# Matmul minus matrix on one core: the last store in three transfers, and the order of SyncE's closing waits

## The chip, the cores and the metric

The kernel runs on one core of one Trainium2 chip. The metric is the device time of one execution in microseconds (us): 209.77 us for the kernel before, as the median of three runs (209.74 to 209.87). The profile is that of one execution; its span, from the first to the last instruction, is 208.0 us, and the run that it was taken of is given with 209.83 us.

## What is computed

```python
x         = (16, 512, 1024) float32
weight    = (1024, 768) float32
sub_value = (16, 512, 768) float32
out = (np.matmul(x, weight) - sub_value).astype(np.float32)
```

So 8192 rows of 1024 are multiplied by one weight, and a matrix of the result's size is subtracted. About 87 MB pass through the DMA engines: x and sub_value in, the result out.

## The kernel before

**Tiles.** The 8192 rows are cut in 64 m tiles of 128 rows. They lie in segments of eight m tiles: within a segment, partition p holds the eight neighbouring rows 8p to 8p+7, and tile j takes row 8p+j of each partition. A transfer of n m tiles therefore moves n x 4,096 bytes of x, or n x 3,072 bytes of sub_value or result, for each of the 128 partitions, as one contiguous piece each.

**Stages.** For each m tile ScalarE casts x to float16 (`cast`, L328), TensorE or VectorE transposes it (L346 and L359, or L379), TensorE multiplies it with the weight in 16 matmuls of 384 columns (`matmuls`, recorded at L199), and VectorE subtracts in place (`finish`, L428): the ring `so_ring` holds sub_value before, and the result after.

**Transfers.** The list `TRANSFERS` orders all loads and stores by hand: `('o', 56, 5), ('o', 61, 2), ('o', 63, 1)` are its last three, the stores of m tiles 56 to 60, of 61 and 62, and of 63. `issue` (L244) works it off whenever a cast or a subtraction is done in program order, and puts every transfer on SyncE's queue, with one exception: the last store is not issued there, but is kept in `outside` (L300).

**Completion.** Every transfer on SyncE takes a semaphore from `lane` (L232), called lane0, lane1 and so on. A lane is used again when it is `known` that all its earlier transfers have landed, because something that was waited for implies it.

**The end.** The instructions are given out engine by engine (L523 to L529) inside a first section that ends with a barrier of the engines. A second section (L532) belongs to SyncE: it waits for every lane whose transfers aren't known to have landed. There are seven of them, of which lane6, the last made, is that of the store of 61 and 62. The build puts them on wait instructions that carry two semaphores each, with the engines' own closing semaphores as partners; the first one is recorded at L535, the others at L567. Behind the section stands the last store, of m tile 63: 128 partitions of 3,072 bytes, issued by ScalarE (L537). `add_manual_dep` puts it behind the section in the order of the program without a semaphore (`NoSync`): as built, its issue waits for the end of the first section, and not for the lanes. SyncE then waits for the last store's own semaphore in a drain, and a closing barrier of all engines ends the program.

Of the kernel before, what the change touches and what calls it, by code (L numbers as in the profile page):

```python
# [8 lines left out]
P = 128  # L9
# [95 lines left out]
def kernel(  # L105
# [7 lines left out]
    nc = tc.nc  # L113
# [7 lines left out]
    n_mt = M_TOT // P  # L121
# [47 lines left out]
    def count(name):  # L169
# [13 lines left out]
        out=along, data0=ones, data1=ones, initial=0.0, op0=mybir.AluOpType.mult, op1=mybir.AluOpType.add,  # L183
    ), waits=[(counter["ident"], 1)], then=count("ident"))
    dve.add(lambda: nc.vector.transpose(across, along), waits=[(counter["ident"], 3)], then=count("ident"))  # L185
    for a in range(P // Q):
        here = slice(a * Q, (a + 1) * Q)
        dve.add(lambda here=here: nc.vector.tensor_tensor(  # L188
            out=ident[here, here], in0=along[here], in1=across[here], op=mybir.AluOpType.is_equal,
# [37 lines left out]
    lanes = []  # L227
    of_x, of_s, of_o = {}, {}, {}
    known = set()
# [300 lines left out]

    section.close()
    with tc.tile_critical(sync_engine=mybir.EngineType.SP, no_gpsimd_drain=True) as waited:  # L532
        for one in lanes:
            if not one["tags"] <= known:
                nc.sync.wait_ge(one["sem"], one["value"])  # L535
    here, there = outside
    stored = nc.scalar.dma_start(out=here, in_=there)  # L537
    tc.add_manual_dep(
        stored.ins, waited.name, mybir.DependencyInfo(mybir.DependencyClass.NoSync, mybir.DependencyReason.DATA),
        reason="behind the waits",  # L540
    )


# [28 lines left out]
```

## Time and profile before

| What | Value |
|---|---|
| time, median of 3 | 209.77 us |
| span of the profiled execution | 208.0 us |
| last subtraction (L428) | 201.44 to 202.40 us |
| last store, issue on ScalarE (L537) | 202.65 us, 0.36 us |
| last store, issue to landing | 4.5 us |
| store of m tiles 61 and 62, issue (L308) | 199.83 us |
| the same, issue to landing | 6.4 us |
| mean DMA rate over the span | 419 GB/s |

The page gives each engine's busy time and share, then the span in 40 slices with the busy share in tenths, where the DMA row is the mean over the core's 16 DMA engines. The chain that ended last is followed back from the last instruction. For an end of a few microseconds these are too coarse: there the timeline, the busy time by stretches that one sets oneself, and the view of what SyncE waited for are to be read. Register, branch, semaphore and DMA-issuing instructions are not counted as busy; a name such as SPq or ACTq is the queue of SyncE or ScalarE.

### The profile page before, as it was taken

The page shows a single profiled execution, that of the slowest core. Times are in us where ns is not written, and L with a number is a line of the kernel's source. Part 1 is how long each engine was busy: PE and PEld are TensorE (multiplying, and loading weights), DVE is VectorE, ACT ScalarE, POOL GpSimd, SP SyncE. Part 2 cuts the span into 40 slices and gives each one's busy share as a digit, 9 for nine tenths or more (in the row PEclk, how much of TensorE's full clock was granted, in tenths as well). Part 3 has the DMA queues.
Part 4 walks back from the last instruction along what each step waited for, and adds up shares of the span by engine and source line. Part 5 has one row for each costly group of instructions (what it writes and reads, how often), then busy time and mean ns, then how long its engine had stood idle before and what let it go on. Part 6 is the DMA issues. An engine that isn't in the chain of part 4 may idle for free.

```text
span 208.0 us, 2608 instructions
## 1 busy us (share of the span) xinstructions
PE 196.5 (94%) x1233; PEld 75.4 (36%) x701; DVE 127.8 (61%) x224; ACT 113.5 (55%) x113; POOL 1.0 (0%) x7
## 2 busy tenths in 40 slices
PE   6989699999999999999999999999999999999970
PEld 0133334333434433443443443344344344334410
DVE  2321516946894795598399379469839937943330
ACT  3274688616673861945745586293664738607300
POOL 1000000000000000000000000000000000000000
PEclk9999999999999999999999999999999999999997
DMA  6999999999999999999999999999999999999993
GB/s 224 405 430 428 429 428 432 443 427 433 449 411 473 376 454 435 463 410 408 474 422 416 421 435 449 405 471 395 444 441 433 428 411 449 444 416 425 423 420 164
DMA packets 4932, 87.08 MB, mean 419 GB/s; under 512 B 576, under 2 KB 576, under 8 KB 960
## 3 DMA queue, kind: packets, MB, share of 16 engines
q1 hardware_dynamic: 4752, 86.64, 97.5%
q10 hardware_dynamic: 176, 0.40, 0.5%
q8 instruction: 1, 0.02, 0.0%
q14 instruction: 3, 0.02, 0.0%
HBM read 61.87 MB, written 25.17 MB: 418 GB/s over the span
## 4 chain that ended last, share of the span: by engine, by line
PE 72%; DMA 22%; ACT 2%; issue 1%; DVE 0%; SPq 0%
PE po_b L199 65%; DMA x_ring<-in_x_dram 22%; PE pt_b L346 7%; ACT x_b L328 1%; DVE so_ring L428 0%; ACT xt_b L359 0%; SPq L265 0%; SPq L308 0%; SPq L567 0%; ACT x16p_b L328 0%; SPq L137 0%
## 5 line engine op out<-in xcount | busy, mean ns | idle before, releaser
L199 PE MATMUL po_b<-w_sb,xt_b 128*128 128x384 f16 x704 | 125.8, 326 | 1.8 <-DVE so_ring L428 1.4
L428 DVE TENSOR_TENSOR so_ring<-po_b,so_ring 128x768 f32<-128x768 f32 x64 | 60.5, 956 | 59.8 <-PE po_b L199 40.0
L359 ACT COPY xt_b<-pt_b 128x1024 f16<-128x1024 f16 x44 | 44.4, 1011 | 61.2 <-PE pt_b L346 61.2
L379 DVE STREAM_TRANSPOSE xtp_b<-x16p_b 32x256 f32<-32x256 f32 x144 | 62.7, 435 | 3.5 <-ACT x16p_b L328 1.4
L199 PE MATMUL po_b<-w_sb,xtp_b 128*128 128x384 f16 x320 | 61.3, 326 | 0.2 <-issue 0.2
L408 PEld LDWEIGHTS <-xt_b 128*128 128x128 f16 x352 | 34.4, 98 | 59.3 <-issue 53.9
L328 ACT CAST x_b<-x_ring 128x1024 f16<-128x1024 f32 x46 | 50.6, 1127 | 8.2 <-DMA x_ring<-in_x_dram 8.2
L346 PE MATMUL pt_b<-ident,x_b 128*128 128x128 f32 x184 | 47.5, 274 | 1.2 <-ACT x_b L328 1.1
L346 PEld LDWEIGHTS pt_b<-ident,x_b 128*128 128x128 f32 x184 | 25.3, 141 | 45.4 <-issue 39.4
L328 ACT CAST x16p_b<-x_ring 128x1024 f16<-128x1024 f32 x18 | 20.2, 1124 | 11.5 <-DMA x_ring<-in_x_dram 11.5
L408 PEld LDWEIGHTS <-xtp_b 128*128 128x128 f16 x160 | 15.6, 97 | 18.6 <-issue 16.5
L199 PE MATMUL po_b<-idle_x,idle_w 128*128 128x512 f16 x25 | 8.8, 505 | 1.7 <-POOL idle_x L179 1.7
L270 DVE CAST w_sb<-so_ring 128x768 f16<-128x768 f32 x8 | 3.9, 555 | 10.1 <-DMA so_ring<-in_weight_dram 10.1
L359 ACT COPY xtp_b<-pt_b 128x1024 f16<-128x1024 f16 x2 | 2.0, 1015 | 1.4 <-PE pt_b L346 1.4
L328 ACT ACT_TABLE_LOAD x1 | 1.3, 1283 | 1.6 <-SPq L137 1.6
L438 PEld LDWEIGHTS <-idle_w 128*128 128x128 f16 x5 | 0.5, 99 | 2.1 <-POOL idle_x L179 1.7
L188 DVE TENSOR_TENSOR ident<-along,across 32x32 f32<-32x32 f32 x4 | 0.7, 183 | 0.1
L180 DVE MEMSET ones<- 128x32 f32 x1 | 0.1, 85 | 1.0 <-SPq L137 1.0
L179 POOL MEMSET idle_x<- 128x512 f16 x1 | 0.5, 528 | 0.0
L510 ACT CAST stub<-ident 128x1 f16<-128x1 f32 x2 | 0.4, 193 | 0.0
L185 DVE STREAM_TRANSPOSE across<-along 128x32 f32<-128x32 f32 x1 | 0.2, 211 | 0.0
L487 POOL MEMSET mark<- 128x1 f32 x1 | 0.1, 98 | 24.9 <-ACT xtp_b L359 24.9
(7 smaller groups left out, 1.0 us busy)
## 6 DMA issues: line engine op xcount, KB each, us to landing
so_ring<-in_sub_value_dram SPq DMA_DIRECT2D x7, 3072.0 KB, 24.4
out_dram<-so_ring SPq DMA_DIRECT2D x7, 3072.0 KB, 26.3
x_ring<-in_x_dram SPq DMA_DIRECT2D x5, 4096.0 KB, 23.1
x_ring<-in_x_dram SPq DMA_DIRECT2D x2, 2048.0 KB, 29.2
so_ring<-in_weight_dram SPq DMA_DIRECT2D x2, 1536.0 KB, 9.6
x_ring<-in_x_dram SPq DMA_DIRECT2D x3, 1024.0 KB, 20.5
so_ring<-in_sub_value_dram SPq DMA_DIRECT2D x2, 1536.0 KB, 23.3
x_ring<-in_x_dram SPq DMA_DIRECT2D x1, 3072.0 KB, 27.4
```

The lines of the kernel that those rows point to most:

```text
L179: pool.add(lambda: nc.gpsimd.memset(idle_x, 0.0), then=count("idle"))
L188: dve.add(lambda here=here: nc.vector.tensor_tensor(out=ident[here, here], in0=along[here], in1=across[here], op=mybir.AluOpType.is_equal, ...
L199: return nc.tensor.add_instruction(mybir.InstMatmult(name=nc.get_next_instruction_name(), engine=full.engine, ins=list(full.ins), outs=lis ...
L270: lambda c=c, r=r, here=here: nc.vector.tensor_copy(out=w_sb[:, c, r], in_=here),
L328: act.add(lambda: nc.scalar.copy(out=to, in_=x_in), waits, count("cast"))
L346: pe.add(lambda: nc.tensor.transpose(words, from_, ident), waits, count("turn") if last else None)
L359: act.add(lambda: nc.scalar.copy(out=to, in_=pt_b[:, b]), waits, count("evac"))
L379: dve.add(lambda: nc.vector.transpose(xt[b * Q : (b + 1) * Q, :, a * Q : (a + 1) * Q], x16[a * Q : (a + 1) * Q, :, b * Q : (b + 1) * Q],), ...
L408: pe.add(lambda weights=weights: nc.tensor.ldweights(weights, tile_position=(0, 0)), [w for w in waits if w[0] in ready])
L428: dve.add(lambda: nc.vector.tensor_tensor(out=o, in0=po[:, :, :NS], in1=o, op=mybir.AluOpType.subtract), [landed["s", mi], (counter["mul"] ...
L438: pe.add(lambda: nc.tensor.ldweights(idle_w, tile_position=(0, 0)), [(counter["idle"], 2)])
L510: lambda t=t: nc.scalar.copy(out=stub[:, t - n_mt : t - n_mt + 1], in_=ident[:, :1]), [(counter["ident"], made)], count("cast")
```

## The change

The last store is issued in three transfers, of partitions 77 to 127 (51), 0 to 63 (64) and 64 to 76 (13), in this order, all on ScalarE. Together they move the same 128 rows to the same place. Its purpose is another spread of the rows over the DMA engines than eight on each. Each of the three has a semaphore of its own, for all of which SyncE waits at the end: two in a wait instruction, and one in the drain.

In SyncE's second section the same seven lanes are waited for, but sorted, so that the one that carries the store of m tiles 61 and 62 (`of_o[n_mt - 2]`) comes first in the list. The build gives the waits out in reverse, here as before, so that it is waited for last. Its purpose is that the other waits be done while that store is under way. In the instructions as built, it moves from the first of six wait instructions to the sixth; PE, DVE and GpSimd have the same instructions as before, and ScalarE has two transfers more.

```diff
     section.close()
     with tc.tile_critical(sync_engine=mybir.EngineType.SP, no_gpsimd_drain=True) as waited:
-        for one in lanes:
-            if not one["tags"] <= known:
-                nc.sync.wait_ge(one["sem"], one["value"])
+        tail = [one for one in lanes if not one["tags"] <= known]
+        tail.sort(key=lambda one: of_o[n_mt - 2] not in one["tags"])
+        for one in tail:
+            nc.sync.wait_ge(one["sem"], one["value"])
     here, there = outside
-    stored = nc.scalar.dma_start(out=here, in_=there)
-    tc.add_manual_dep(
-        stored.ins, waited.name, mybir.DependencyInfo(mybir.DependencyClass.NoSync, mybir.DependencyReason.DATA),
-        reason="behind the waits",
-    )
+    for rows in (slice(77, P), slice(0, 64), slice(64, 77)):
+        stored = nc.scalar.dma_start(out=here[rows], in_=there[rows])
+        tc.add_manual_dep(
+            stored.ins, waited.name, mybir.DependencyInfo(mybir.DependencyClass.NoSync, mybir.DependencyReason.DATA),
+            reason="behind the waits",
+        )
 
 
 # ---- launch: one core; inputs and outputs as the reference has them ----
```

## The prediction

> **What bounds the kernel now.** I read the page first, then the end of the span by stretches, then SyncE's own waits, then the DMA queues of the last 12 us. Page, parts 1, 2 and 4:
>
> ```profile
> PE 196.5 (94%) x1233; PEld 75.4 (36%) x701; DVE 127.8 (61%) x224; ACT 113.5 (55%) x113; POOL 1.0 (0%) x7
> ...
> DMA  6999999999999999999999999999999999999993
> ...
> PE 72%; DMA 22%; ACT 2%; issue 1%; DVE 0%; SPq 0%
> ```
>
> TensorE is busy nearly throughout and the DMA engines are full up to the last slice. But the diff touches nothing before the last store, so only what lies after the last subtraction counts. The timeline from 202 us on has just two entries:
>
> ```profile
> 201.44 0.96 DVE L428 TENSOR_TENSOR so_ring<-po_b,so_ring 128x768 f32<-128x768 f32 x1 [1.64 <-PE po_b L199]
> 202.65 0.36 ACTq L537 DMA_DIRECT2D out_dram<-so_ring  x1
> ```
>
> Arithmetic ends at 202.40 us and the span at 208.0: 5.6 us are transfer and closing waits. The same stretch in the table by stretches (columns: stretch, its length, busy time of PE, PEld, DVE, ACT, POOL, granted clock, DMA share of 16 engines, GB/s):
>
> ```profile
> 203.50:204.00 0.50, 0.00 (x0) 0.00 (x0) 0.00 (x0) 0.00 (x0) 0.00 (x0) 1.00 0.87 350
> 204.00:204.50 0.50, 0.00 (x0) 0.00 (x0) 0.00 (x0) 0.00 (x0) 0.00 (x0) 1.00 1.03 418
> 204.50:205.00 0.50, 0.00 (x0) 0.00 (x0) 0.00 (x0) 0.00 (x0) 0.00 (x0) 1.00 0.34 135
> 205.00:205.40 0.40, 0.00 (x0) 0.00 (x0) 0.00 (x0) 0.00 (x0) 0.00 (x0) 0.50 0.22 92
> 205.40:205.80 0.40, 0.00 (x0) 0.00 (x0) 0.00 (x0) 0.00 (x0) 0.00 (x0) 0.50 0.15 61
> 205.80:206.20 0.40, 0.00 (x0) 0.00 (x0) 0.00 (x0) 0.00 (x0) 0.00 (x0) 0.50 0.14 54
> 206.20:206.60 0.40, 0.00 (x0) 0.00 (x0) 0.00 (x0) 0.00 (x0) 0.00 (x0) 0.50 0.13 54
> 206.60:207.00 0.40, 0.00 (x0) 0.00 (x0) 0.00 (x0) 0.00 (x0) 0.00 (x0) 0.50 0.02 8
> ```
>
> Read the DMA share. 0.13 is two engines of sixteen: most are done by 204.8, three still work after 205, two until 206.8. Those two end the kernel. The packet records give their times. Twelve engines start their eight rows of the last store between 203.53 and 203.84, one at 204.12, one at 204.92, and the two latest, called A and B here, at 205.70 and 205.85, each right after its share of the store of m tiles 61 and 62. Packets of 3,072 bytes follow each other every 0.118 us, so eight rows take 0.94 us: B's end at 206.79. Its completion is recorded at 207.14, 0.35 later, SyncE's drain starts at 207.16, and 0.86 us of closing barrier follow. The row price can be seen in the DMA queues of 196 to 208 us, too:
>
> ```profile
> q10 hardware_dynamic: 144, 0.39, 8.1%
> ```
>
> 8.1% of 16 engines over 12 us is 15.6 engine-us; over 128 rows it is 0.12 each. Last, SyncE's own waits:
>
> ```profile
> SPq L535 <- DMA out_dram<-so_ring: 3.5, 1, 3.5
> ...
> SPq L567 <- DMA out_dram<-so_ring: 0.2, 1, 0.2
> ```
>
> The 3.5 is the wait for the store of 61 and 62, which lands at 206.19. Only 0.2 us is left for the last store. Between the two, SyncE's instruction records show six semaphore waits 0.06 us apart (206.21 to 206.51), a branch, an increment, a drain and a no-op until 206.90. So a last store that landed earlier would gain just those 0.2 us as the waits stand now. That is why the diff has its other half.
>
> [...] 51 partitions go on 3 engines (17 rows each), 64 on 16 (4 each), 13 on 13 (1 each). The trace agrees for 128 only: 16 engines with eight rows; it holds no odd count, so this is the unproven step. [...] the trace shows unequal engines but not their numbers. [...] four packets of kind "instruction" after the start (one of 16 KB, 0.94 us; three of 8 KB, 0.31 us each). Following back-to-back packets, A's lag appears at two of these, B's mostly at one (35.3 us), while the engine at 204.92 falls behind gradually from 120 us. So the lags come with the program and should be there after the change.
>
> **The change, part by part.** (1) Three transfers for one. Rows by engine: 17+4+1 = 22 on engines 0 to 2, 4+1 = 5 on 3 to 12, 4 on 13 to 15, in place of eight everywhere.
> If B is one of 13 to 15: rows end at 205.85 + 4 x 0.118 = 206.32, and land at 206.67, 0.47 earlier.
> A with five rows and a second completion packet (0.015): 205.70 + 0.59 + 0.015 = 206.31, landing 206.66; with four, earlier still.
> Engines 0 to 2, if ordinary: 203.53 to 203.84 + 22 x 0.118 + 0.02 = 206.14 to 206.45, landing 206.5 to 206.8, typically 206.6. So they lie just beneath B, and could pass it only from the latest ordinary start.
> (2) Issue: two more of 0.36 us on ScalarE, at about 203.0 and 203.4, so rows follow 0.5 us later (as 203.53 follows 203.01), the last about 204.3. A and B do not reach them before 205.7, and engines 0 to 2 have 17 rows to work on until 205.5: hidden. ScalarE has nothing after them but the barrier, which SyncE reaches far later.
> (3) Waits: each transfer has its own semaphore, so SyncE ends with a two-semaphore wait and then its drain, in place of the drain alone. I take the spacing of such waits, 0.065 us, as it lies behind the landing; bounds 0 (if the transfer awaited by the drain lands last) and 0.13.
> (4) The sorted waits: the one for 61 and 62 moves from the first to the sixth of the wait instructions. Behind it now stand five, 0.31 us; then none. SyncE is ready for the last store at 206.90 - 0.31 = 206.6 plus one step of 0.06, just before 206.67. Nothing else on SyncE waits behind it but the end. The other five semaphores have long arrived, so sorting costs nothing.
> Sum: -0.47 + 0.065 = -0.41 us, 209.77 to 209.36.
>
> **The rivals.**
> Ordinary placement: B is one of engines 3 to 12 and gets five rows: its end moves by 3 x 0.118 - 0.015 = 0.34, less 0.065: 209.50. The trace numbers no engine, so it speaks neither for nor against this.
> Slower: one of the late engines is among the lowest three and gets 22 rows. The engine at 204.92 would land at 204.92 + 2.60 + 0.02 + 0.35 = 207.89: +0.75 + 0.065, 210.6. A or B would land at 208.7 or 208.8, giving 211.4. For it: 3 of 16 places, three late engines, a blind draw would put one there in nearly half the cases. [...] the trace cannot settle it.
> No change: [...] 51 rows spread over 13 engines by four; A or B then keeps up to nine rows: 209.8. About the same if the engine at 204.12 is among the lowest three: 204.12 + 2.62 + 0.35 = 207.09.
> More gain: the added wait hides (bound 0) or landing latency shrinks with half the rows: 209.30 or a little less.
>
> **How the numbers follow.** Main case 0.50, more gain 0.15, five rows for B 0.10, no change 0.05, slower 0.20 [...]. 0.2% is 0.42 us, right on the main case; I give about half of it (0.27) to faster. Faster 0.27 + 0.15 = 0.42; same 0.23 + 0.10 + 0.05 = 0.38; slower 0.20. The range goes from 209.25 (the more-gain case) to 210.0, past the no-change case with its bounds; the slower cases at 210.6 and 211.4, 0.20 in all, are left out.
>
> **What would show it.** In the table by stretches, 205.0 to 206.1 should have a share of five or six engines (0.31 to 0.37: A, B, the three lowest, until 205.5 the gradual one too) where it is about 0.15 to 0.2 now, and be empty after 206.4. The wait for 61 and 62 should still end near 206.2, and that for the last stores near 206.7. The prediction is wrong if some engine still moves rows at 207 (a late engine among the lowest three), if the rows are not 17, 4 and 1 by engine, or if SyncE's closing waits end well after the landing.

## The result and the profile after

The changed kernel takes 210.67 us (median of six runs, 210.47 to 210.93), the kernel before 209.82 us beside it. The ratio is 1.0043, 95% interval 1.003 to 1.0056: slower by 0.9 us (0.6 to 1.2). The forecast was 209.36 us, faster.

The profiled execution has a span of 208.6 us, against 208.0. First the two entries of its timeline after 201.7 us:

```profile
201.72 0.96 DVE L428 TENSOR_TENSOR so_ring<-po_b,so_ring 128x768 f32<-128x768 f32 x1 [1.64 <-PE po_b L199]
202.92 1.96 ACTq L539 DMA_DIRECT2D out_dram<-so_ring  x3
```

The three issues together take 1.96 us with the gaps between them; I had counted 3 x 0.36. Their single durations, in the instruction records of line 539, are 0.54, 0.52 and 0.83 us. Now the end by stretches (columns as in the prediction; the last two are the DMA share and GB/s):

```profile
203.50:204.00 0.50, 0.00 (x0) 0.00 (x0) 0.00 (x0) 0.00 (x0) 0.00 (x0) 1.00 0.44 166
204.00:204.50 0.50, 0.00 (x0) 0.00 (x0) 0.00 (x0) 0.00 (x0) 0.00 (x0) 1.00 0.46 154
204.50:205.00 0.50, 0.00 (x0) 0.00 (x0) 0.00 (x0) 0.00 (x0) 0.00 (x0) 1.00 0.77 147
205.00:205.40 0.40, 0.00 (x0) 0.00 (x0) 0.00 (x0) 0.00 (x0) 0.00 (x0) 1.00 0.74 207
205.40:205.80 0.40, 0.00 (x0) 0.00 (x0) 0.00 (x0) 0.00 (x0) 0.00 (x0) 1.00 0.99 269
205.80:206.20 0.40, 0.00 (x0) 0.00 (x0) 0.00 (x0) 0.00 (x0) 0.00 (x0) 1.00 0.56 185
206.20:206.60 0.40, 0.00 (x0) 0.00 (x0) 0.00 (x0) 0.00 (x0) 0.00 (x0) 1.00 0.30 115
206.60:207.00 0.40, 0.00 (x0) 0.00 (x0) 0.00 (x0) 0.00 (x0) 0.00 (x0) 0.59 0.21 85
207.00:207.40 0.40, 0.00 (x0) 0.00 (x0) 0.00 (x0) 0.00 (x0) 0.00 (x0) 0.50 0.04 15
```

Read share and rate together (a row is one partition's packet of 3,072 bytes). Before, a share of 1.03 moved 418 GB/s. Here, from 204.5 to 205.8, shares of 0.74 to 0.99 move only 147 to 269: the engines are busy with rows that take longer. And the end is no longer two engines at 0.13, but three to five until 207.0. The queue of the last store says the same for the whole of it, over 12 us (196.5 to 208.5):

```profile
q10 hardware_dynamic: 160, 0.39, 12.6%
```

12.6% of 16 engines over 12 us is 24.2 engine-us for the same 128 rows, 0.19 each, where it was 0.12. SyncE's own waits:

```profile
SPq L569 <- DMA out_dram<-so_ring: 4.0, 3, 1.8
```

All waits for stores stand in one line now. By the instruction records, that for the store of m tiles 61 and 62 ends at 206.21, the no-op behind it is at 206.59 (it was 206.90: the sorting did what it was to do), and the wait for the last stores ends at 207.70. The landing records show what it waited for. The one store of before has 16 entries there, and its queue 16 packets of 4 bytes beside the 128 rows. The three transfers have 34 entries and 32 such packets (160 in all with the rows); the two entries over come at 203.54 and 205.05, ahead of the first of the 32 (205.87). The others are read here as one for each engine of the transfer:

```
transfer        completions (us)
51 partitions   early entry at 203.54, then 206.78, 206.85, 207.04
64 partitions   eleven from 206.22 to 206.38, then 206.69, 207.04, 207.25, 207.33, 207.52
13 partitions   early entry at 205.05, eight from 206.37 to 206.56,
                then 206.86, 207.22, 207.42, 207.50, 207.69
```

Behind the early entries these are 3, 16 and 13 engines, the counts that the prediction took for 51, 64 and 13 partitions and that the trace of before didn't show. The last three engines to land are those with 17 + 4 + 1 rows. Their 17 rows end in the packet records at 206.44, 206.52 and 206.70, 3.5 to 3.8 us after the issue; five rows more at 0.118 end at 207.04, 207.12 and 207.30. The two lagging engines (those that are latest before the last store, as A and B were) moved five rows each and landed at 206.86 and 207.22. So it is not a lagging engine that ends this kernel.

### The profile page after: what moved, and what is told of

Its sections match the earlier page's. It is cut to its first block, busy times and chain, and to the rows that moved or that the text cites. A ratio compares the mean times of both kernels' runs of the same rounds, so it can differ in the third digit from the quotient of the medians.

```text
span 208.6 us, 2611 instructions
## 1 busy us (share of the span) xinstructions
PE 195.5 (94%) x1233; PEld 75.6 (36%) x701; DVE 128.0 (61%) x224; ACT 113.4 (54%) x113; POOL 1.0 (0%) x7
## 4 chain that ended last, share of the span: by engine, by line
PE 75%; DMA 14%; DVE 6%; SPq 2%; issue 1%; DVEq 0%
PE po_b L199 67%; DMA so_ring<-in_sub_value_dram 14%; PE pt_b L346 8%; DVE xtp_b L379 3%; DVE so_ring L428 2%; SPq L308 1%; SPq L265 0%; SPq L569 0%; DVEq L58 0%; SPq L137 0%
## 5 line engine op out<-in xcount | busy, mean ns | idle before, releaser
L328 ACT CAST x16p_b<-x_ring 128x1024 f16<-128x1024 f32 x18 | 20.2, 1122 | 11.4 <-DMA x_ring<-in_x_dram 11.4
L199 PE MATMUL po_b<-idle_x,idle_w 128*128 128x512 f16 x25 | 8.0, 464 | 1.7 <-POOL idle_x L179 1.7
```

The source lines that it names most:

```text
L199: return nc.tensor.add_instruction(mybir.InstMatmult(name=nc.get_next_instruction_name(), engine=full.engine, ins=list(full.ins), outs=lis ...
L328: act.add(lambda: nc.scalar.copy(out=to, in_=x_in), waits, count("cast"))
```

## The experiments

Three theories went to the chip. PORTS: the pace of the rows depends on which partitions a transfer takes (the name is a guess of the author's at the cause, which no run here shows). FEED: transfers on few engines or of odd counts are issued and fed slowly. LATE: a lagging engine is among the lowest three after all, which are the three engines of the 51 partitions. Four more (DEPTH and WHOLE, LAG and PATH) are told in the expectations where they were tried. Each piece of code below shows the lines that differ; in all kernels the rest is that of the changed kernel.

### Each half of the change alone

```diff
-    for rows in (slice(77, P), slice(0, 64), slice(64, 77)):
+    for rows in (slice(0, P),):
```

> One store of 128 partitions as before, with the sorted waits: half of the change alone. Theories on the changed kernel: PORTS ([...] rows take 0.24 us instead of 0.12), FEED (transfers on 3 and 13 engines are issued and fed slowly), LATE (a lagging engine is among the lowest three). All three expect the same here: SyncE is ready at 206.6 instead of 206.9, the store still lands 0.35 us after its last row on the latest engine (207.1), so the time is that of before within 0.1 us.

Measured: ratio to before 1.0000 (0.9992 to 1.0009). The no-op behind SyncE's waits is at 206.61, the last landing at 207.17. As all expected.

```diff
-        tail.sort(key=lambda one: of_o[n_mt - 2] not in one["tags"])
```

> The three transfers of 51, 64 and 13 with the waits in the old order: the other half alone. The three landings of the changed kernel end at 207.7, later than SyncE's 206.9 with old waits, so all theories expect the whole loss here: 0.7 to 0.9 us above before, within 0.1 us of the changed kernel.

Measured: ratio 1.0042 (1.0029 to 1.0056), the changed kernel's own loss. So the whole loss comes with the three transfers, and the sorting is worth nothing as long as the last store lands after 206.9.

### Is it the partitions? Halves, and a middle

```diff
-    for rows in (slice(77, P), slice(0, 64), slice(64, 77)):
+    for rows in (slice(0, 64), slice(64, P)):
```

> Two transfers of 64 partitions (0 to 63, 64 to 127), both on 16 engines with four rows each, sorted waits; each engine has eight rows as before. PORTS: rows on engines that work at the same time take 0.22 to 0.24 us in both halves; the two latest engines, which work nearly alone, still take 0.12, and end as before, so the time is before's plus 0.07 (an added wait) to 0.2. FEED: both transfers are on 16 engines, so rows take 0.12 and issues 0.36 us each; time before plus 0.07. LATE: as FEED.

```diff
-    for rows in (slice(77, P), slice(0, 64), slice(64, 77)):
+    for rows in (slice(32, 96), slice(0, 32), slice(96, P)):
```

> Three transfers on 16 engines each: partitions 32 to 95 (four rows each), 0 to 31 (two), 96 to 127 (two), sorted waits. PORTS: [...] its rows take 0.12 us, and those of the other two 0.24; FEED and LATE: all 0.12. Time by all: before plus 0.07 to 0.2 us, as the latest engines have eight rows as before. Issue of three transfers on 16 engines: FEED expects 3 x 0.36 = 1.1 us where 51, 64 and 13 took 1.96 with the gaps.

Two transfers of 64 partitions, both first in their kernel, both on 16 engines with four rows of 3,072 bytes each (the last store's queue has 160 packets with two transfers and 176 with three: 128 rows, and 16 more for each transfer): 0 to 63 in one, 32 to 95 in the other. By stretches, from the first rows of the halves on:

```profile
204.15:204.65 0.50, 0.00 (x0) 0.00 (x0) 0.00 (x0) 0.00 (x0) 0.00 (x0) 1.00 1.09 276
204.65:205.15 0.50, 0.00 (x0) 0.00 (x0) 0.00 (x0) 0.00 (x0) 0.00 (x0) 1.00 0.84 234
```

and from the first rows of the middle on:

```profile
204.45:204.95 0.50, 0.00 (x0) 0.00 (x0) 0.00 (x0) 0.00 (x0) 0.00 (x0) 0.50 1.03 418
204.95:205.45 0.50, 0.00 (x0) 0.00 (x0) 0.00 (x0) 0.00 (x0) 0.00 (x0) 0.50 0.88 246
205.45:205.95 0.50, 0.00 (x0) 0.00 (x0) 0.00 (x0) 0.00 (x0) 0.00 (x0) 0.50 0.71 203
```

The middle runs at full rate, 0.12 us a row, in the first line; then come the two quarters, most of whose rows take 0.17 to 0.24 us. Partitions 0 to 63 are slow from the beginning: most of their rows take 0.19 to 0.24 us, 0.225 on the mean until 205.0. So far the pace depends on which partitions they are, as PORTS expected for these two; by what cause is not shown. The second half, 64 to 127, was mixed, 0.12 to 0.24, which PORTS alone did not expect, and so were the quarters.

Yet both kernels take before's time: 1.0002 (0.9993 to 1.0011) and 1.0006 (0.9997 to 1.0014). More transfers and slower rows cost nothing in these two, where each engine still has eight rows, as ordinary engines have the time. Issues took 0.45 to 0.62 us each, for 64 as for 32 partitions; my 0.36 holds for 128.

### Is it the 17 rows on one engine?

```diff
-    for rows in (slice(77, P), slice(0, 64), slice(64, 77)):
+    for rows in (slice(77, P),):
```

> Of the last store only the transfer of partitions 77 to 127 on 3 engines is issued; partitions 0 to 76 of m tile 63 are left out. In the changed kernel its 17 rows per engine took 2.6 to 2.8 us from the first row, 0.16 each, not 0.118. PORTS: [...] the other two transfers read other partitions; so most of the slowness stays: 2.4 to 2.8 us. FEED: the rows stalled because the next two transfers were being issued; alone, 17 rows take 17 x 0.118 = 2.0 us.

```diff
-    for rows in (slice(77, P), slice(0, 64), slice(64, 77)):
+    for rows in (slice(38, 89),):
```

> As the run with 51 partitions alone, but partitions 38 to 88, [...]; the other 77 partitions of m tile 63 are left out. PORTS: 17 rows in 2.0 us, 0.118 each, against 2.4 to 2.8 for 77 to 127. FEED: 2.0 us in both.

```diff
-    for rows in (slice(77, P), slice(0, 64), slice(64, 77)):
+    for rows in (slice(77, 94),):
```

> Of the last store only partitions 77 to 93 are issued, [...]; the other 111 partitions of m tile 63 are left out. With 51 partitions alone on three engines, the fifth to seventh rows of each engine stalled for 0.2 to 0.5 us each, [...]. DEPTH (the stall comes with many rows on one engine of a transfer): the same stalls here, 17 rows take 2.5 us or more. WHOLE (it comes with the feed of the whole transfer of 51 rows): few or none here, 17 rows in 2.0 to 2.2 us.

```diff
-    for rows in (slice(77, P), slice(0, 64), slice(64, 77)):
+    for rows in (slice(0, 119),):
```

> Of the last store only partitions 0 to 118 are issued, [...]; partitions 119 to 127 of m tile 63 are left out. The lagging engines 3 and 4 are among them, so the ordinary ones are read. DEPTH: 17 rows take about as long as with three engines, 2.5 to 2.8 us. WHOLE: the feed of 119 rows takes twice as long as that of 51, so that the rows stall until some 4 us after the issue.

The queue of the last store over the same 12 us; in order: 51 rows from partition 77, 51 from 38, 17 rows, 119 rows:

```profile
q10 hardware_dynamic: 54, 0.16, 4.1%
```

```profile
q10 hardware_dynamic: 54, 0.16, 4.2%
```

```profile
q10 hardware_dynamic: 18, 0.05, 1.4%
```

```profile
q10 hardware_dynamic: 126, 0.37, 10.5%
```

Beside their rows these queues have 3, 3, 1 and 7 packets, by the reading above one for each engine of the transfer. 7.9, 8.1, 2.7 and 20.2 engine-us: 0.154, 0.158, 0.158 and 0.17 us a row. The first three are alike, with 51 rows from either place, and even with one engine alone. And from its issue to its last landing the transfer of partitions 77 to 127 took 4.08 us alone, against 4.12 in the changed kernel, so the two transfers behind it did not slow it. The slowness of these rows is in the transfer itself: PORTS, which expected 0.118 us a row for partitions 38 to 88, does not explain it, and neither does the issue of the next transfers, as FEED had it. The single engine's packets show where it lies:

```
start of rows (us; in brackets the duration where over 0.13 us):
204.264 (0.135)  204.405 (0.239)  204.659 (0.342)  204.998  205.116  205.233 (0.205)
205.472 (0.352)  205.821, then every 0.118 until 206.879
```

About 0.7 us are lost in the first seven rows; after that the pace is 0.118. The 51 rows show it too, with single rows of up to 0.54 us, most of it within 2.6 us of the issue. But not every engine stalls, as the expectation for the 17 rows took it: of the three engines of partitions 38 to 88, the one that began its rows last, 1.5 us after the issue, lost nothing. With 119 rows on seven engines, followed from packet to packet, the five ordinary engines take 2.6 to 4.3 us for 17 rows, with long rows until 4.4 us after the issue; the two lagging ones, which begin more than 2.2 us after it, take the plain 2.0. So neither DEPTH nor WHOLE holds as it stood. That late beginners lose nothing points to rows that are fed slowly at first, but this is not shown. Why these transfers stall, while one of 128 partitions (eight rows each) and one of partitions 32 to 95 on 16 engines run without a stall (0.118 us a row), stays open. It was not tried whether rows of another size stall as long.

### Which engines lag?

The trace numbers no engine. The numbers here are places: engine k works in the transfers on k + 1 or more engines, and in none on fewer. In the changed kernel the three engines of the 51 partitions are also among the 13: the last three landings of the three transfers follow each other by the same 0.47 to 0.48 and 0.17 us. For the transfers below it is taken as given, and not shown, that the fewer engines are always among the more. Then an engine of a lower place moves more rows, and the rows and landings of the three lagging ones (A, B and the gradual one of the prediction) narrow down their places.

```diff
-    for rows in (slice(77, P), slice(0, 64), slice(64, 77)):
+    for rows in (slice(0, 96), slice(96, 107), slice(107, 116), slice(116, 123), slice(123, P)):
```

> Five transfers of 96, 11, 9, 7 and 5 partitions. [...] LATE: one of them has ten, and is among 0 to 2. PORTS and FEED: the two latest are among 3 to 12, as in the changed kernel they moved five rows each, so 7 to 9 (or 6 for 11 and 12).

```diff
-    for rows in (slice(77, P), slice(0, 64), slice(64, 77)):
+    for rows in (slice(0, 88), slice(88, 100), slice(100, 110), slice(110, 118), slice(118, 124), slice(124, P)):
```

> Six transfers of 88, 12, 10, 8, 6 and 4 partitions. [...] With the run of odd counts this names the lagging engines. LATE: 13 rows on one of them. [...]

Lagging engines among the landings of each transfer, by the number of engines that it runs on (one landing each, as read above):

```
engines of the transfer        4   5   6   7   8   9  10  11  12
lagging engines among them     1   2   2   2   2   2   2   3   3
```

The counts never fall, as the places want it. One more lagging engine comes in at five, at eleven and at none between, so two of them are 4 and 10. The third is one of 0 to 3. It is 3, as no lagging engine in the changed kernel could have moved 22 rows in the time: of the three, the first to land its share of the store of m tiles 61 and 62 did so at 205.61; 22 rows more at 0.118 would land at 208.2, and the last landing is at 207.69. LATE falls. Engine 10 is mostly the last, engine 3 the second; engine 4 is the one that falls behind gradually; they are 1.2 to 2.7 us behind the others at the end.

### What sets the end?

```diff
     assert not todo
     marks[n_mt] = len(pe.ops)
+    act.add(lambda: nc.scalar.copy(out=x16_b[:, 0, :640], in_=xt_b[:, 0, :640]), [(counter["finish"], so_far["finish"])])
```

The added copy delays the issue. With one store of 128 partitions:

> A copy of 640 columns on ScalarE (about 0.65 us) is put between the last subtraction and the end of the first section, so that the last store is issued some 0.65 us later; one store of 128 partitions, sorted waits. Theory LAG (the end of the kernel before is set by the two latest DMA engines, whatever the issue time, with some 1.4 us between the ordinary engines' landing and the latest's): no change against before, within 0.15 us. Rival PATH (the end follows the issue of the last store): 0.65 us slower than before.

and with the three transfers:

> The same delay of about 0.65 us in the changed kernel with its three transfers. Theory LAG plus a new bound: with three transfers the three lowest engines end 4.8 us after the issue, later than the lagging ones, so the end now follows the issue: 0.65 us slower than the changed kernel, about 1.5 us above before. Rival (the loss is a fixed cost behind the lagging engines): the changed kernel's time within 0.15 us, 0.85 us above before.

One store, timeline and the end by stretches:

```profile
202.88 0.72 ACT L520 COPY x_b<-xt_b 128x640 f16<-128x640 f16 x1 [5.12 <-DVE so_ring L428]
203.73 0.36 ACTq L540 DMA_DIRECT2D out_dram<-so_ring  x1
```

```profile
205.80:206.20 0.40, 0.00 (x0) 0.00 (x0) 0.00 (x0) 0.00 (x0) 0.00 (x0) 0.50 0.14 54
206.20:206.60 0.40, 0.00 (x0) 0.00 (x0) 0.00 (x0) 0.00 (x0) 0.00 (x0) 0.50 0.13 54
206.60:207.00 0.40, 0.00 (x0) 0.00 (x0) 0.00 (x0) 0.00 (x0) 0.00 (x0) 0.50 0.08 31
```

The store is issued 1.08 us later than in the profile of before, and the end has the same picture: two engines, 0.13. Measured: ratio 0.9999 (0.9989 to 1.0008). So a delay of 0.65 us in the last store's issue costs the kernel with one store nothing: LAG holds, PATH falls.

Three transfers:

```profile
203.46 1.93 ACTq L540 DMA_DIRECT2D out_dram<-so_ring  x3
```

```profile
206.60:207.00 0.40, 0.00 (x0) 0.00 (x0) 0.00 (x0) 0.00 (x0) 0.00 (x0) 0.50 0.26 100
207.00:207.40 0.40, 0.00 (x0) 0.00 (x0) 0.00 (x0) 0.00 (x0) 0.00 (x0) 0.50 0.19 77
207.40:207.80 0.40, 0.00 (x0) 0.00 (x0) 0.00 (x0) 0.00 (x0) 0.00 (x0) 0.50 0.14 54
```

Now the work of about three engines (0.19, three sixteenths) reaches into what was empty. Put together, from six profiles:

```
                           issue     last landing   from issue to landing
before                     202.65    207.14         4.50
one store, sorted          203.38    207.17         3.79
one store, delayed         203.73    207.31         3.58
changed kernel             202.92    207.69         4.76
three, old waits           203.00    207.77         4.77
three, delayed             203.46    208.23         4.77
```

In these profiles one store lands near 207.2 whenever it is issued; three land 4.77 us after the issue. In times, the delayed three took 1.0048 (1.0029 to 1.0068) of before, some 1.0 us (0.6 to 1.4). The 1.5 that I had expected lies just above this interval, and the 0.85 of the rival, a fixed cost behind the lagging engines, lies in it: the times do not show that the delay is passed on in full. The profiles speak for it. In that of the delayed three the issue came 0.54 us later than in the changed kernel and the landing 0.55 later, while the lagging engines finished the store of m tiles 61 and 62 only 0.29 later (206.50 against 206.21).

## Why the prediction was wrong

**The bound of before: right.** Two lagging engines set the end; halves, middle and delay leave the time as it was, and sorting alone gives nothing.

**Rows by engine: right**, 17 + 4 + 1, 4 + 1 and 4. Engines 3 and 10 both had five rows, so the placement with five rows was the true one, and with the prices used it would have given 209.50.

**"Engines 0 to 2 ... landing 206.5 to 206.8": the step that failed.** It had them just beneath B; they became the bound. From issue to landing it counted 3.9 to 4.2 us (from 202.65), and 4.76 was measured. The term that was mis-sized is the row price of 0.118 for the 17 rows. It was taken from a transfer of 128 partitions; in the 51 they took (3.78 - 0.79) / 17 = 0.18 on the slowest engine, counted from the first row at 0.79 to the last engine's end of them at 3.78 us after the issue. My highest value for that point, 1.19 + 17 x 0.118 = 3.2, is short by 0.6 us. The five rows behind (0.6) and the landing (0.38, counted 0.35) were right. With the issue at 202.65 as counted, 4.77 us put the last landing at 207.42: with the added wait a loss of 0.35 us where a gain of 0.41 was forecast. Why the rows are slow stays open.

**Where the rest comes from.** I read the issue time off one profile, 202.65, and asked only whether engines 0 to 2 would then be done in time. In the 11 other profiles without an added copy, whose kernels are the same up to there, it lay between 202.92 and 203.52; the mean of all 12 is 203.14. For the kernel before this does not matter, as the delay showed; for one that ends 4.77 us after the issue it does. As an estimate, 203.14 + 4.77 = 207.91 is 0.60 to 0.77 later than the landings of the one store (207.31 to 207.14); with the added wait, 0.07, that is 0.67 to 0.84 us, within the 0.6 to 1.2 measured. The one profile of the changed kernel alone, with its early issue, accounts for 0.63 us of span.

**The issue, called hidden: wrong by its size.** 1.96 us with gaps, not 1.1; and the first rows of the 64 partitions began 1.2 us after their own issue. The halves and the middle have such issues too and lose nothing by them, so by itself this is not the loss.

**The lagging engines' own gain: smaller than counted.** With five rows, B would have landed at 206.80. The later of the two landed at 207.22, as its first three rows took 0.34, 0.22 and 0.17 us, in the transfer of 64 partitions of one half. That is no earlier than the 207.14 of before, so in this profile there would have been no gain even with quick engines 0 to 2; with the old waits the later one landed at 206.92. All this was hidden behind the lowest three.

**The waits: right.** The added wait took 0.068 us (0.065 counted), and SyncE was ready at 206.6.

**The rivals.** The slower one gave 210.6 for a lagging engine among the lowest three. The number fits by luck; the reason doesn't, as the lagging engines are 3, 4 and 10. The sign given for it, an engine that still moves rows at 207, came true too, though engines 0 to 2 were not late ones.

## What to carry to other kernels

When work is moved off the last finisher, the engine that takes it needs its own full account: its row price in the new kind of transfer, and the start time over several executions, since its end may follow something else (here the issue) than the old bound did. A transfer of fewer partitions isn't a piece of one of 128: depending on which partitions it has and how they are split, its rows came here at the full pace (0.118 us, partitions 32 to 95), at about half of it (0.225 on the mean, 0 to 63), or with stalls (0.15 to 0.17 on the mean, single rows of up to 0.8, with 17 rows an engine). And a delay put on purpose ahead of a step tells cheaply whether that step still has slack.

## What the runs showed of the hardware

- A transfer of 128 partitions of 3,072 bytes is issued by ScalarE in 0.36 us, and its rows come 0.85 to 0.9 us after the issue began. For 96 partitions the issue took 0.37 us; for 51 and 64, 0.50 to 0.62; for 13 and 11, behind others, 0.8; for 12, and for 10 and fewer, behind others, 0.29 to 0.60.
- Sixteen engines on partitions 0 to 63 move most rows in 0.19 to 0.24 us, on 32 to 95 in 0.118.
- Transfers on one, three or seven engines with 17 rows each have long rows, of up to 0.8 us, in the first 2.3 to 4.4 us from the issue; after that their rows follow every 0.118 us. By the busy time of the queue this costs 0.6 to 0.8 us an engine on the mean, and single engines from nothing to about 2.3.
- In these runs DMA engines 3, 4 and 10, numbered by place as above, are 1.2 to 2.7 us behind the others at the end. In before, the lags of the two latest step up where instruction packets of 8 and 16 KB pass: behind that of 16 KB at 35.3 us, the last landing of a transfer goes from 0.16 us after the middle one of its 16 (at 33 us) to 1.42 (at 37 us); behind one of 8 KB at 50.6 us, the second last goes from 0.10 to 1.02. The two runs that number the engines have the same two steps (1.4 to 1.6 us at 33 us, 0.8 to 0.9 at 55), and both engines stay behind until the end, so that 10 and 3 are the engines of these packets if the two keep their order.
